# FoX/MLA hybrid layer on one core: projection tiles spread among the heads, first norm and tail reordered, and half of the output projection moved among the MLA heads

## The chip, the cores and the metric

One Trainium2 chip, one of its cores. The time is device microseconds of one execution; several runs are made and their median is given. Engines: TensorE (PE, its weight loads PEld), VectorE (DVE), ScalarE (ACT), GpSimd (POOL) and SyncE (SP), whose queue issues most transfers.

## What is computed

One inference step of one layer over T = 576 columns: 512 frames of a new stream ("prompt") and 64 frames of a running one ("sample", with 1024 cached positions). Model width 1024.

```python
z = rmsnorm(x, g_attn) @ w_in      # FoX q|k|v (512 each), forget logits (8), MLA q-latent (384), kv-latent (256), rope key (32)
fox = softmax(q k^T / 8 + F[t] - F[s], causal) v          # 8 heads x 64, F = cumsum(log sigmoid(f + b))
mla = softmax((q_lat c^T + q_rope k_rope^T) / sqrt(96), chunk-causal) c @ w_uv    # 8 heads
x = x + concat[fox, mla] @ w_out
u = causal_conv3(rmsnorm(x, g_ffn) @ w_up)
x = x + (silu(u_gate) * u_val) @ w_down                   # D_FF = 2816
y = rmsnorm(x, final_norm)
```

Outputs are y and the new state: FoX k, v and log forget values, the normalised kv-latent, the rotated key, and the last convolution rows.

## The kernel before

Everything lies transposed: features on the 128 partitions, the 576 columns along the free axis, x as eight tiles. Operands of the large products are split into a high and a low part (float32r), and a product is three matmuls: low x high, high x high, high x low. Weights come by `wload` (L183): a transfer into one of two "wr" buffers, a ScalarE copy to the high part and a subtraction for the low part (`hilo`, L192) into one of two "wh" buffers. The subtraction's engine is picked by cycling through a string of `ENG` (L54): "v" VectorE, "g" POOL; the first W0 - 1 calls go to VectorE. `gemm` (L201) works in two column halves (`HA`: 288 + 288) into two PSUM banks, so a tile of 1024 input rows is 48 matmuls. `evac` (L213) takes the two banks out on VectorE.

Buffers are named by tag with a fixed number of each: "raw" 7 (L94), "mix" 8 (L97), "xs" 8 split operands (L100), "wr" and "wh" 2; PSUM has banks g 2, s 3, t 2, o 1.

Stages:
1. x is loaded, scaled and split (`split_scaled`); the rope key with the forget logits, and the first key tile, go through TensorE while ScalarE squares x (L318). Squares are added in two groups of four by the engines of "acc0", column sums over a matrix of ones give the sum of squares, and `rstd` (L260) makes R. `consts` (L176) loads a constant block and copies its parts on VectorE. The projections are scaled by R when they are evacuated.
2. Heads come in pairs p (heads 2p, 2p+1). `fox_gemm` (L447) makes key, query and value tile of a FoX pair, three "raw" buffers. `latent` (L538) makes one of five latent tiles, `latent_norm` (L544) normalises them, `gates` (L559) makes the cumulated forget values from the logits on 8 partitions, with "raw" buffers. `mla_up` (L657) makes queries, keys and values of an MLA pair.
3. Per head: stacked operands by SyncE transfers (`stack`, L470), scores, softmax, transposes, values. Per pair: scores and values of the sample stream. Results are the eight "mix" tiles, FoX 0 to 3 and MLA 4 to 7.
4. Output projection (L859): all eight mix tiles are split, then eight tiles of 48 matmuls, added to x.
5. FFN norm (L871 to L878), 44 up-projection tiles with convolution (`up_conv`, L881), products, and down-projections in four groups; the last one in column halves of 320 and 256 (L959), each with its own norm and output transfers. Its factors are multiplied by POOL in the first half and by POOL or VectorE (`TPOOL`) in the second.

The order of stages 2 and 3 is written by five generators (`s_values`, `s_scores`, `s_sample_values`, `s_sample_scores`, `s_gemm`), each of which yields either ("after", event, latency), to wait, or ("done", cost, event), after it has emitted work. A small planner (L835) always goes on with the generator that is due first on its own clock. The program order so made sets priorities; a scheduler then orders each engine's queue by them and by when operands and buffers are expected to be free. `tc.issue_after(ins)` puts what is emitted in its block behind `ins` on the same engine.

Of the kernel before, what the change touches and what calls it, by code (L numbers as in the profile page):

```python
# [55 lines left out]
    "sq0": "a", "acc0": "gggvvv", "sq": "agv", "acc": "gvvv",  # L56
# [9 lines left out]
TPOOL = (0, 1)  # L66

W0 = 6
# [3 lines left out]
def build(nc, tc, io):  # L72
# [3 lines left out]
    psp = es.enter_context(tc.tile_pool(name="ps", bufs=1, space=PSUM))  # L76

# [5 lines left out]
    def sb(shape, dt, tag, bufs, name=None):  # L83
        return pool.tile(shape, dt, tag=tag, bufs=bufs, name=name or tag)
# [91 lines left out]
    def consts():  # L176
        nc.sync.dma_start(con[:, :N_CON], io["con"])
        V.tensor_copy(ident, con[:, K_ID:K_ID + P])
        V.tensor_copy(bfc, con[:, 0:320])
        V.tensor_copy(sel, con[0:72, K_SEL:K_SEL + 8])  # L180
# [69 lines left out]
    def rstd_of(v, y, a, out):  # L250
        S.activation(y, v, AF.Ln)
        S.activation(y, y, AF.Exp, scale=-0.5)
        newton(v, y, a, out)

    def newton(v, y, a, out):
        V.tensor_tensor(a, y, y, op=ALU.mult)
        V.scalar_tensor_tensor(a, a, -0.5, v, op0=ALU.mult, op1=ALU.mult)
        V.scalar_tensor_tensor(out, a, 1.5, y, op0=ALU.add, op1=ALU.mult)

    def rstd(ps, n, out):  # L260
        v, y, a = (raw()[:, :T] for _ in range(3))
        evac(lambda d, p, c: V.tensor_scalar(d, p, 1.0 / n, EPS, op0=ALU.mult, op1=ALU.add), v, ps)
        rstd_of(v, y, a, out)
# [52 lines left out]
    with tc.issue_after(ends[0]), tc.issue_after(ends[1]):  # L316
        consts()
        rstd(col_sums([sq_sum([t[:, :T] for t in x_in[n:n + 4]], "sq0", "acc0") for n in (0, 4)]), D, R)  # L318
# [128 lines left out]
    def fox_gemm(p):  # L447
        ps = k0 if p == 0 else in_tile(p)
        k = raw()
        evac(lambda d, p, c: V.tensor_tensor(d, p, R[:, c], op=ALU.mult), k, ps)  # L450
        G.dma_start(io["o_k"][p], k[:, :T])
        ps = in_tile(4 + p)
        q = raw()
        evac(lambda d, p, c: V.scalar_tensor_tensor(d, p, FOX_SCALE, R[:, c], op0=ALU.mult, op1=ALU.mult), q, ps)
        ps = in_tile(8 + p)
# [3 lines left out]
        return q, k, v  # L459
# [96 lines left out]
    fx = {0: fox_gemm(0)}  # L556
    gate = {}

    def gates():  # L559
        S.activation(z, z, AF.Identity, bias=bf)  # L560
        mn = raw()[:8, :T]
        V.scalar_tensor_tensor(mn, z, -1.0, z, op0=ALU.mult, op1=ALU.min)
        e = raw()[:8, :T]
        S.activation(e, mn, AF.Exp)
        up = raw()[:8, :T]
# [5 lines left out]
        logf = raw()[:8, :T]  # L571
# [4 lines left out]
        fp = raw()[:8, :T]  # L576
# [162 lines left out]

    done = {("x", 0): 0.0}  # L740
    clock = [0.0]

    def s_gemm():
        for p in range(1, 4):
            if p >= 2:
                yield ("after", ("stack", 2 * (p - 2) + 1), 0)
            fx[p] = fox_gemm(p)
            if p == 1:
                gates()
            yield ("done", 23.1, ("up", p))  # L750
            if p == 1:
                for a in range(5):
                    latent(a)
                    if a == 2:
                        rope_key()
                    if a == 1:
                        acc_c = sq_sum(craw)
                    if a == 4:
                        acc_q = sq_sum(qcr)
                    yield ("done", 7.7, ("lat", a))  # L760
            if p == 2:
                latent_norm(craw, 256, C_GKV, acc_c)
                latent_norm(qcr, 384, C_GQ, acc_q)
                for a in range(2):
                    G.dma_start(io["o_lat"][a], craw[a])
        mla_keys()
        yield ("done", 0, ("keys", 0))
        for p in range(4):
            if p == 0:
                yield ("after", ("stack", 5), 0)  # L770
            else:
                yield ("after", ("stack", 6 + 2 * p - 1), 0)
            if p % 2 == 0:
                q_rope(p // 2)
                yield ("done", 2.2, ("rope", p))
            mla_up(p)
            yield ("done", 5, ("up", 4 + p))

# [99 lines left out]
    rstd(sumsq(x2), D, R2)  # L878
    cs = sb([P, 512], F32, "KR", 1)[:, :176].rearrange("p (a b) -> p a b", b=4)

    def up_conv(ch):  # L881

        hl = wload(io["w_up"][ch], 1024)
        ps = psg()
        gemm(ps, P, hl, x2hl, HB)
# [17 lines left out]
    def g_tile():  # L903
# [9 lines left out]
        return t[0][:, k * 1152:(k + 1) * 1152].rearrange("p (a b) -> p a b", a=2)  # L913

# [44 lines left out]
    for hf, (o, w) in enumerate(HC):  # L959
# [138 lines left out]
```

## Time and profile before

| | us |
|---|---|
| median of 3 runs (lowest, highest) | 809.66 (807.43, 810.17) |
| the profiled execution | 810.69 |
| its span, first to last instruction | 808.9 |
| TensorE matmuls / weight loads busy | 772.8 / 743.3 |
| VectorE / ScalarE / POOL busy | 508.5 / 340.6 / 264.0 |

Times are microseconds from the span's start; a row of a stage table gives the length of the stretch, then each engine's busy time in it with its number of instructions. A row of a timeline gives start, duration, engine, line, operation, tiles out<-in, shapes, count, and in brackets the idle time before it and what ended it. Neighbouring instructions of one kind are merged into a row, so its duration can hold short waits. Weight loads overlap matmuls. Full clock is 1.00, the lower of the two levels 0.50.

### The profile page before, as it was taken

The page shows a single profiled execution, that of the slowest core. Times are in us where ns is not written, and L with a number is a line of the kernel's source. Part 1 is how long each engine was busy: PE and PEld are TensorE (multiplying, and loading weights), DVE is VectorE, ACT ScalarE, POOL GpSimd, SP SyncE. Part 2 cuts the span into 40 slices and gives each one's busy share as a digit, 9 for nine tenths or more (in the row PEclk, how much of TensorE's full clock was granted, in tenths as well). Part 3 has the DMA queues.
Part 4 walks back from the last instruction along what each step waited for, and adds up shares of the span by engine and source line. Part 5 has one row for each costly group of instructions (what it writes and reads, how often), then busy time and mean ns, then how long its engine had stood idle before and what let it go on. Part 6 is the DMA issues. An engine that isn't in the chain of part 4 may idle for free.

```text
span 808.9 us, 14256 instructions
## 1 busy us (share of the span) xinstructions
PE 772.8 (96%) x5582; PEld 743.3 (92%) x5582; DVE 508.5 (63%) x941; ACT 340.6 (42%) x611; POOL 264.0 (33%) x390
## 2 busy tenths in 40 slices
PE   8898999999899989999999999999999999999994
PEld 8796899897789879999999999999999999999993
DVE  6838554878677763457867524676425667675356
ACT  7224652457667864124443212343113433433231
POOL 5134342336143230223333221433222343332034
PEclk9998999999999999999999999999999999999997
DMA  9373423545563741222222223222232222222313
GB/s 329 111 212 109 109 84 106 145 107 169 129 152 80 185 131 30 80 79 79 72 85 68 79 92 105 79 79 60 79 98 80 103 80 79 79 66 83 105 40 117
DMA packets 33811, 83.98 MB, mean 104 GB/s; under 512 B 6006, under 2 KB 9350, under 8 KB 33744
## 3 DMA queue, kind: packets, MB, share of 16 engines
q1 hardware_dynamic: 31520, 78.55, 32.6%
q0 software_dynamic: 1008, 3.19, 1.1%
q10 hardware_dynamic: 1216, 1.33, 0.5%
q8 instruction: 44, 0.72, 0.4%
q14 instruction: 23, 0.19, 0.1%
HBM read 64.12 MB, written 5.49 MB: 86 GB/s over the span
## 4 chain that ended last, share of the span: by engine, by line
PE 76%; DVE 10%; ACT 5%; DMA 3%; issue 3%; SPq 1%; POOL 1%; DVEq 0%; ACTq 0%; POOLq 0%
PE g L210 31%; PE s L210 19%; PE t L210 12%; PE g L438 3%; PE g L969 1%; DMA mix<-xT 1%; DVE B L382 1%; DVE xs L267 1%; PE s L720 1%; PE t L375 1%; ACT p L326 1%; PE s L969 1%; DMA A<-qr 1%; PE s L522 1%; DVE raw L135 1%
## 5 line engine op out<-in xcount | busy, mean ns | idle before, releaser
L210 PE MATMUL g<-xs,wh 128*128 128x288 f32 (+2 forms) x2028 | 281.1, 295 | 0.3 <-ACT spt L128 0.2
L210 PEld LDWEIGHTS g<-xs,wh 128*128 128x128 f32 x2028 | 271.1, 189 | 1.7 <-ACT spt L128 0.4
L194 ACT ACTIVATE wh<-wr 128x1024 fp32r<-128x1024 f32 (+4 forms) x106 | 99.8, 942 | 204.3 <-PE g L210 88.4
L135 POOL TENSOR_TENSOR wh<-wr,wh 128x1024 fp32r<-128x1024 f32 (+3 forms) x51 | 111.8, 2192 | 216.5 <-ACT wh L194 173.7
L210 PE MATMUL s<-xs,wh 128*128 128x320 f32 (+3 forms) x840 | 121.1, 300 | 2.3 <-DVE xs L267 2.3
L210 PEld LDWEIGHTS s<-xs,wh 128*128 128x128 f32 (+1 forms) x840 | 116.3, 188 | 2.7 <-ACT wh L194 1.8
L210 PE MATMUL t<-xs,wh 128*128 128x256 f32 (+3 forms) x576 | 83.9, 296 | 1.2 <-DVE xs L267 1.2
L210 PEld LDWEIGHTS t<-xs,wh 128*128 128x128 f32 (+1 forms) x576 | 79.1, 188 | 1.6 <-DVE xs L267 1.4
L135 DVE TENSOR_TENSOR wh<-wr,wh 128x1024 fp32r<-128x1024 f32 (+5 forms) x55 | 59.0, 1077 | 13.7 <-ACT wh L194 13.4
L892 POOL COPY KR<-raw 128x2 f32<-128x2 f32 x33 | 14.6, 443 | 94.1 <-DVE raw L890 94.1
L332 POOL TENSOR_SCALAR p<-p,small 128x128 f32<-128x128 f32 (+2 forms) x48 | 27.5, 575 | 50.9 <-DVE small L327 40.8
L896 DVE SCALAR_TENSOR_TENSOR raw<-raw,par 128x578 f32<-128x578 f32 x22 | 33.6, 1526 | 14.0 <-ACT raw L895 14.0
L326 ACT ACTIVATE p<-s,small 128x128 f32<-128x128 f32 (+1 forms) x64 | 33.6, 527 | 12.5 <-DVE small L361 9.2
L920 ACT ACTIVATE raw<-raw 128x578 f32<-128x578 f32 x22 | 15.1, 688 | 54.5 <-DVE raw L897 54.5
L382 DVE TENSOR_TENSOR B<-t,B 128x512 fp32r<-128x512 f32 (+1 forms) x64 | 29.9, 482 | 9.3 <-ACT B L128 9.2
L128 ACT ACTIVATE B<-t 128x512 fp32r<-128x512 f32 (+1 forms) x64 | 26.2, 435 | 17.1 <-PE t L375 16.4
L361 DVE TENSOR_REDUCE small<-s 128x1 f32<-128x128 f32 (+1 forms) x64 | 30.5, 480 | 4.3 <-PE s L359 2.9
L896 DVE SCALAR_TENSOR_TENSOR raw<-pq,par,raw 128x578 f32<-128x578 f32 x11 | 22.7, 2059 | 12.4 <-ACT raw L895 12.4
L375 PE MATMUL t<-ident,p 128*128 128x128 f32 x160 | 29.1, 277 | 1.0 <-DVE B L382 0.5
L890 DVE TENSOR_TENSOR raw<-s,R 128x256 f32<-128x256 f32 x22 | 9.3, 424 | 31.8 <-PE s L210 31.8
L438 PE MATMUL g<-spt,sv 128*128 128x128 f32 x216 | 26.7, 276 | 0.3 <-ACT spt L128 0.2
L438 PEld LDWEIGHTS g<-spt,sv 128*128 128x128 f32 x216 | 25.2, 192 | 1.1 <-ACT spt L128 0.6
(337 smaller groups left out, 1344.1 us busy)
## 6 DMA issues: line engine op xcount, KB each, us to landing
wr<-w_up SPq DMA_DIRECT2D x44, 512.0 KB
wr<-w_dn SPq DMA_DIRECT2D x24, 384.0 KB
wr<-w_in SPq DMA_DIRECT2D x16, 512.0 KB
A<-pq SPq DMA_DIRECT2D x32, 256.0 KB
mix<-xT SPq DMA_DIRECT2D x16, 288.0 KB
wr<-w_out SPq DMA_DIRECT2D x8, 512.0 KB
A<-pq SPq DMA_DIRECT2D x24, 128.0 KB
sk<-k_c SPq DMA_DIRECT2D x4, 512.0 KB
```

What stands on the lines that cost most here:

```text
L128: S.activation(dst, src, AF.Copy)
L135: (V if pick(kind) == "v" else G).tensor_tensor(dst, a, b, op=op)
L194: S.activation(hl[:, 0, a:b], r[:, a:b], AF.Copy)
L210: PE.matmul(ps[hf][:M, :w], lhsT=hl[:, wi, kc * M:(kc + 1) * M], rhs=acts[kc][:, xi, o:o + w], start=(kc == 0 and pi == 0), stop=(kc == n ...
L326: S.activation(p, src, AF.Exp, bias=nm, accum_out=sm[:, 0:1])
L332: (G if e == "g" else V).tensor_scalar(p, p, sm[:, 1:2], 1.0, op0=ALU.mult, op1=ALU.mult)
L361: V.reduce_max(nm[:, 0:1], s[:, :W], axis=AX.X, negate=True)
L375: PE.transpose(t[:, P * (i - j):P * (i - j + 1)], st["p"][i][:, P * j:P * (j + 1)], ident)
L382: V.tensor_tensor(ptj[:, 1, off:], t[:, :w], f(ptj[:, 0, off:]), op=ALU.subtract)
L438: PE.matmul(out, lhsT=v[:, j, :], rhs=spt[:, j, :], start=(j == 0), stop=(j == 8))
L896: V.scalar_tensor_tensor(t, u[:, 1:579], par[:, C_CW + 44 + ch:C_CW + 44 + ch + 1], t, op0=ALU.mult, op1=ALU.add)
L969: PE.matmul(ps[:, :w], lhsT=whl[m][:, wi, kc * P:(kc + 1) * P], rhs=g2[kc][:, xi, c], start=(kc == 0 and pi == 0), stop=(kc == n - 1 and p ...
```

## The change

- `s_gemm` emits projection tiles one at a time, each a step of 6.4 on the planner's clock (before: a pair's three tiles at once for 23.1, a latent tile 7.7), in the order F1, two latent tiles, F2, three latent tiles, F3 (F1 is the second FoX pair). The gates come after pair 1's key tile. Both latent norms come after F3.
- The gates' small tiles are "mix" buffers instead of "raw".
- First norm: all six additions of squares on VectorE, the three constant copies behind the norm, W0 5 instead of 6.
- Output projection: after the last MLA up-projection, FoX head 7 and the fourth sample pair, `s_gemm` splits mix tiles 0 to 3 and emits eight half tiles (24 matmuls each) that add x and store the partial sum in device memory; behind the heads, eight half tiles with mix 4 to 7 load the partial sums and add them.
- FFN: the first gate tile and the first value tile run through their eight input blocks together, with the sum of squares placed after four of them.
- Tail: POOL takes four tiles of the first column half and three of the second; in the second half the factor stays in PSUM for VectorE and ScalarE copies it for POOL.

```diff
-    "sq0": "a", "acc0": "gggvvv", "sq": "agv", "acc": "gvvv",
+    "sq0": "a", "acc0": "v", "sq": "agv", "acc": "gvvv",
...
-TPOOL = (0, 1)
-W0 = 6
+TPOOL = ((0, 1, 2, 3), (0, 1, 2))
+W0 = 5
...
     def consts():
         nc.sync.dma_start(con[:, :N_CON], io["con"])
-        V.tensor_copy(ident, con[:, K_ID:K_ID + P])
-        V.tensor_copy(bfc, con[:, 0:320])
-        V.tensor_copy(sel, con[0:72, K_SEL:K_SEL + 8])
...
-        rstd(col_sums([sq_sum([t[:, :T] for t in x_in[n:n + 4]], "sq0", "acc0") for n in (0, 4)]), D, R)
+        normed = rstd(col_sums([sq_sum([t[:, :T] for t in x_in[n:n + 4]], "sq0", "acc0") for n in (0, 4)]), D, R)
+    with tc.issue_after(normed):
+        V.tensor_copy(ident, con[:, K_ID:K_ID + P])
+        V.tensor_copy(bfc, con[:, 0:320])
+        V.tensor_copy(sel, con[0:72, K_SEL:K_SEL + 8])
...
     def gates():
         S.activation(z, z, AF.Identity, bias=bf)
-        mn = raw()[:8, :T]
+        mn = mixt()[:8]
...
+    def out_half(m):
+        hl = wload(io["w_out"][m][:, :512], 512)
+        xm = mixt()
+        nc.sync.dma_start(xm, io["xT"][:, m, :])
+        ps = psg()
+        gemm(ps, P, hl, mhl[:4], HA)
+        evac(lambda d, p, c: V.tensor_tensor(d, p, d, op=ALU.add), xm, ps)
+        nc.sync.dma_start(parts[m], xm)
...
     def s_gemm():
...
+        acc = {}
+        for what in ("F1", "l0", "l1", "F2", "l2", "l3", "l4", "F3"):
+            n = int(what[1])
+            if what[0] == "F":
+                if n >= 2:
+                    yield ("after", ("stack", 2 * (n - 2) + 1), 0)
+                for j, _ in enumerate(fox_gemm(n)):
+                    if n == 1 and j == 0:
+                        gates()
+                    yield ("done", 6.4, ("part", n))
+                yield ("done", 0, ("up", n))
+            else:
+                latent(n)
...
+                yield ("done", 6.4, ("lat", n))
+        latent_norm(craw, 256, C_GKV, acc["c"])
+        latent_norm(qcr, 384, C_GQ, acc["q"])
...
             mla_up(p)
             yield ("done", 5, ("up", 4 + p))
+        yield ("after", ("o", 7), 0)
+        yield ("after", ("so", 3), 0)
+        mhl.extend(split(t) for t in mixes[:4])
+        for m in range(8):
+            out_half(m)
+            yield ("done", 3.2, ("out", m))
...
-    mhl = [split(t) for t in mixes]
+    mhl.extend(split(t) for t in mixes[4:])
     x2 = []
     for m in range(8):
-        hl = wload(io["w_out"][m], 1024)
+        hl = wload(io["w_out"][m][:, 512:], 512)
         xm = mixt()
-        nc.sync.dma_start(xm, io["xT"][:, m, :])
+        nc.sync.dma_start(xm, parts[m])
         ps = psg()
-        gemm(ps, P, hl, mhl, HA)
+        gemm(ps, P, hl, mhl[4:], HA)
...
-    rstd(sumsq(x2), D, R2)
+    def up_gemm(chs):
+        hls = [wload(io["w_up"][ch], 1024) for ch in chs]
+        pss = [psg() for _ in chs]
+        for kc in range(8):
+            if kc == 4:
+                rstd(sumsq(x2), D, R2)
+            for hl, ps in zip(hls, pss):
+                for hf, (o, w) in enumerate(HB):
+                    for pi, (wi, xi) in enumerate(((0, 1), (0, 0), (1, 0))):
+                        PE.matmul(ps[hf][:, :w], lhsT=hl[:, wi, kc * P:(kc + 1) * P], rhs=x2hl[kc][:, xi, o:o + w],
+                                  start=(kc == 0 and pi == 0), stop=(kc == 7 and pi == 2))
+        return dict(zip(chs, pss))
...
+    early.update(up_gemm((0, NCH)))
...
-        newton(v, y, a, r3)
+        if hf:
+            newton(v, y, a, pn[:, :w])
+            S.activation(r3, pn[:, :w], AF.Copy)
+            r3, r3g = pn[:, :w], r3
+        else:
+            newton(v, y, a, r3)
+            r3g = r3
...
-                if hf == 0 or m in TPOOL:
+                if m in TPOOL[hf]:
                     G.tensor_scalar(x2[m][:, c], x2[m][:, c], gl, 1.0, op0=ALU.mult, op1=ALU.mult)
-                    G.tensor_tensor(yt[:, j], x2[m][:, c], r3, op=ALU.mult)
+                    G.tensor_tensor(yt[:, j], x2[m][:, c], r3g, op=ALU.mult)
```

## Rows read from the trace of the kernel before

**Rows 1.** The page, busy time of each engine over the span.
```profile
PE 772.8 (96%) x5582; PEld 743.3 (92%) x5582; DVE 508.5 (63%) x941; ACT 340.6 (42%) x611; POOL 264.0 (33%) x390
```

**Rows 2.** Stage table: length; busy PE, PEld, DVE, ACT, POOL; PE clock, DMA share, GB/s.
```profile
20.00:41.00 21.00, 18.07 (x109) 16.01 (x109) 17.12 (x23) 6.49 (x11) 4.22 (x4) 0.92 0.37 120
...
69.00:78.00 9.00, 6.05 (x23) 4.43 (x24) 7.43 (x22) 4.68 (x11) 4.46 (x5) 0.68 0.21 66
78.00:104.00 26.00, 24.63 (x171) 21.14 (x170) 15.22 (x47) 18.29 (x49) 12.13 (x21) 0.98 0.46 111
104.00:146.00 42.00, 42.00 (x319) 41.76 (x318) 20.48 (x34) 13.01 (x24) 14.32 (x14) 1.00 0.34 101
146.00:180.00 34.00, 33.16 (x232) 30.17 (x231) 29.42 (x59) 17.82 (x38) 12.70 (x16) 1.00 0.43 121
180.00:212.00 32.00, 28.66 (x186) 23.25 (x185) 27.89 (x67) 24.50 (x66) 15.52 (x22) 1.00 0.64 170
212.00:268.00 56.00, 52.12 (x340) 46.58 (x340) 38.07 (x98) 38.16 (x95) 17.05 (x26) 1.00 0.47 121
268.00:318.00 50.00, 46.38 (x328) 41.79 (x326) 33.10 (x91) 33.02 (x84) 12.19 (x20) 1.00 0.41 114
...
369.00:381.00 12.00, 10.82 (x83) 10.62 (x83) 10.53 (x13) 5.80 (x8) 3.34 (x5) 1.00 0.19 61
```

**Rows 3.** Timelines of the first norm: DVE, ACT, POOL and PE, 13 to 31 us.
```profile
18.71 5.67 DVE L135 TENSOR_TENSOR raw<-raw 128x576 f32<-128x576 f32 x3
...
30.29 0.72 DVE L256 TENSOR_TENSOR raw<-raw 128x576 f32<-128x576 f32 x1
...
13.94 4.69 ACT L220 ACTIVATE raw<-mix 128x576 f32<-128x576 f32 x8
19.11 2.25 ACT L194 ACTIVATE wh<-wr 128x1024 fp32r<-128x1024 f32 x2 [0.48 <-PE t L210]
...
21.43 2.34 POOL L135 TENSOR_TENSOR wh<-wr,wh 128x1024 fp32r<-128x1024 f32 x1 [0.68 <-ACT wh L194]
...
24.44 3.24 PE L230 MATMUL s<-raw,ones 128*128 128x288 f32 x6 [2.89 <-DVE raw L135]
27.07 1.03 PE L210 MATMUL g<-xs,wh 128*128 128x288 f32 x2
```

**Rows 4.** Timelines of the gates: ACT, DVE, and the PE wait at their end.
```profile
35.20 0.76 ACT L560 ACTIVATE mix<-mix,bf 8x576 f32<-8x576 f32 x1
...
59.34 0.74 DVE L562 SCALAR_TENSOR_TENSOR raw<-mix 8x576 f32<-8x576 f32 x1
...
71.79 0.90 PE L523 MATMUL s<-cf,sl 72*128 72x384 f32 x3 [3.13 <-DVE cf L590]
```

**Rows 5.** Latent norms, last FoX tile and head 8's first score (PE timeline; line L548).
```profile
145.44 0.65 PE L230 MATMUL g<-raw,ones 128*128 128x288 f32 x2
...
177.98 1.85 PE L210 MATMUL g<-xs,wh 128*128 128x288 f32 x12
...
212.53 0.28 PE L701 MATMUL s<-A 128*128 128x256 f32 x1
...
L548 DVE SCALAR_TENSOR_TENSOR mix<-mix,par,raw x5: 802/805/810, 157.0 to 164.4; 128x576 f32<-128x576 f32 x5
```

**Rows 6.** Last up-projection, output projection and its evacuations; SyncE's queue.
```profile
268.17 1.64 PE L668 MATMUL g<-xs,wh 128*128 128x512 f32 x6
...
318.41 51.13 PE L210 MATMUL g<-xs,wh 128*128 128x288 f32 x384
...
L867 DVE TENSOR_TENSOR mix<-g,mix x16: 442/458/459, 323.8 to 370.2; 128x288 f32<-128x288 f32 x16
...
266.90 8.48 SPq L185 DMA_DIRECT2D wr<-w_out  x3
```

**Rows 7.** The tail: final products of VectorE (line L996), an addition of squares.
```profile
L996 DVE SCALAR_TENSOR_TENSOR pq<-mix,par,v x2: 473/706/940, 802.3 to 803.2; 128x256 f32<-128x256 f32 x2
...
796.05 1.02 DVE L978 TENSOR_TENSOR raw<-raw 128x256 f32<-128x256 f32 x1 [0.48 <-ACT raw L976]
```

More of the change, by code (lines that the diff above doesn't have):

```diff
@@ L76, in build @@
     psp = es.enter_context(tc.tile_pool(name="ps", bufs=1, space=PSUM))
+    dram = es.enter_context(tc.tile_pool(name="hbm", bufs=1, space=bass.MemoryType.DRAM))
     V, S, G, PE = nc.vector, nc.scalar, nc.gpsimd, nc.tensor
@@ L252, in rstd_of @@
         S.activation(y, y, AF.Exp, scale=-0.5)
-        newton(v, y, a, out)
+        return newton(v, y, a, out)
     def newton(v, y, a, out):
@@ L257, in newton @@
         V.scalar_tensor_tensor(a, a, -0.5, v, op0=ALU.mult, op1=ALU.mult)
-        V.scalar_tensor_tensor(out, a, 1.5, y, op0=ALU.add, op1=ALU.mult)
+        return V.scalar_tensor_tensor(out, a, 1.5, y, op0=ALU.add, op1=ALU.mult).ins
     def rstd(ps, n, out):
@@ L262, in rstd @@
         evac(lambda d, p, c: V.tensor_scalar(d, p, 1.0 / n, EPS, op0=ALU.mult, op1=ALU.add), v, ps)
-        rstd_of(v, y, a, out)
+        return rstd_of(v, y, a, out)
     def split_scaled(dst, src, g):
@@ L451, in fox_gemm @@
         G.dma_start(io["o_k"][p], k[:, :T])
+        yield
         ps = in_tile(4 + p)
@@ L454, in fox_gemm @@
         evac(lambda d, p, c: V.scalar_tensor_tensor(d, p, FOX_SCALE, R[:, c], op0=ALU.mult, op1=ALU.mult), q, ps)
+        yield
         ps = in_tile(8 + p)
@@ L458, in fox_gemm @@
         G.dma_start(io["o_v"][p], v[:, :T])
-        return q, k, v
+        fx[p] = q, k, v
+        yield
     def pair_split(q, k):
@@ L554, in split @@
         return t
-    fx = {0: fox_gemm(0)}
+    fx = {}
+    for _ in fox_gemm(0):
+        pass
     gate = {}
@@ L560, in gates @@
         S.activation(z, z, AF.Identity, bias=bf)
-        mn = raw()[:8, :T]
+        mn = mixt()[:8]
         V.scalar_tensor_tensor(mn, z, -1.0, z, op0=ALU.mult, op1=ALU.min)
-        e = raw()[:8, :T]
+        e = mixt()[:8]
         S.activation(e, mn, AF.Exp)
-        up = raw()[:8, :T]
+        up = mixt()[:8]
         V.tensor_scalar(up, e, 1.0, None, op0=ALU.add)
@@ L570, in gates @@
         V.tensor_tensor(up, up, e, op=ALU.add)
-        logf = raw()[:8, :T]
+        logf = mixt()[:8]
         V.scalar_tensor_tensor(logf, z, 0.0, up, op0=ALU.min, op1=ALU.subtract)
@@ L575, in gates @@
         G.memset(zero8, 0.0)
-        fp = raw()[:8, :T]
+        fp = mixt()[:8]
         V.tensor_tensor_scan(fp[:, :NP], logf[:, :NP], zero8[:, :NP], 0.0, op0=ALU.add, op1=ALU.add)
@@ L737, in mla_sample_values @@
         yield 0.4
+    mhl = []
+    parts = [dram.tile([P, T], F32, tag=f"part{m}", bufs=1, name=f"part{m}") for m in range(8)]
+    def out_half(m):
[6 more added lines that the diff above has]
+        nc.sync.dma_start(parts[m], xm)
     done = {("x", 0): 0.0}
@@ L743, in s_gemm @@
     def s_gemm():
[L744 to L765, printed above, removed]
+        acc = {}
[11 more added lines that the diff above has]
+                latent(n)
+                if n == 2:
+                    rope_key()
+                if n == 1:
+                    acc["c"] = sq_sum(craw)
+                if n == 4:
+                    acc["q"] = sq_sum(qcr)
+                yield ("done", 6.4, ("lat", n))
+        latent_norm(craw, 256, C_GKV, acc["c"])
+        latent_norm(qcr, 384, C_GQ, acc["q"])
+        for a in range(2):
+            G.dma_start(io["o_lat"][a], craw[a])
         mla_keys()
@@ L877, in build @@
     R2 = sb([P, T], F32, "R", 1)
-    rstd(sumsq(x2), D, R2)
     cs = sb([P, 512], F32, "KR", 1)[:, :176].rearrange("p (a b) -> p a b", b=4)
-    def up_conv(ch):
-        hl = wload(io["w_up"][ch], 1024)
-        ps = psg()
-        gemm(ps, P, hl, x2hl, HB)
+    def up_gemm(chs):
[10 more added lines that the diff above has]
+        return dict(zip(chs, pss))
+    early = {}
+    def up_conv(ch):
+        ps = early.pop(ch, None)
+        if ps is None:
+            hl = wload(io["w_up"][ch], 1024)
+            ps = psg()
+            gemm(ps, P, hl, x2hl, HB)
         u = raw()
```

## The prediction

> **What bounds the kernel now.** I read the page's busy times first: TensorE's matmuls are busy 96% of the span and its weight loads 92%, VectorE 63% [rows 1]. So TensorE is the bound, and only the time in which it does not load weights can be won. The table by stage says where that is [rows 2]. Idle weight-load time is the stretch less its PEld column: 5.0 us in 20 to 41, 4.6 in 69 to 78, 4.9 in 78 to 104, 3.8 in 146 to 180, 8.8 in 180 to 212, 9.4 in 212 to 268, 8.2 in 268 to 318, 1.4 in 369 to 381; 104 to 146 is the control, dense at 319 matmuls in 42 us (0.132 us each). The output projection is dense too, 384 matmuls in 51.13 us [rows 6]. From the stretches with idle time I went to the timelines for what is late there.
>
> [...] By the PE column the stages from 78 to 318 hold 13.1 us of idle time where PEld shows 35.1; the sum below, made from PE, would be about 15 us instead of 20.
>
> **The change, part by part.** Durations are those of the profiled execution: 810.7 us, a span of 808.9 and 1.8 around it. The median of the runs is 809.7, 1.0 lower.
>
> *First norm.* The last ScalarE square ends at 18.6 [rows 3]. Three adds on VectorE then take 5.67 us between POOL adds, though an operation of that kind and shape takes 0.72 alone [rows 3]; the column sums wait until 24.44, run at half clock (the granted clock of 20 to 41 is 0.92 [rows 2]), and the query tile of pair 0 starts only at 27.07. With all six adds on VectorE the last ends near 18.6 + 0.7 = 19.4. Next late are that tile's weights: their subtraction moves from VectorE to POOL (W0 is 5), from about 20.2, after ScalarE's copy, for 2.34 us [rows 3]; the tile starts near 22.8. **-4.3 us**; bounds 0 (POOL is held up by the norm's Newton steps) and -5. The three constant copies move behind the norm: short, and nothing before head 0 reads them. The alternation of later subtractions between POOL and VectorE shifts by one call: nothing, their number stays.
>
> *Gates and tile by tile.* ScalarE adds the forget bias at 35.20, but the next step of the chain starts at 59.34 [rows 4]. It needs a "raw" buffer, and seven are taken by q, k, v of two pairs. TensorE finally waits 3.1 us for the chain's end [rows 4]; 69 to 78 then does 23 matmuls in 9 us at a mean clock of 0.68 [rows 2], so at the lower of the two levels for most of it, after the idle stretch. With "mix" buffers (free once x is squared and split) the chain, 12.4 us from 59.34 to 71.79, starts near 31 and ends near 43, long before the next three tiles are done. The 23 matmuls cost 3.0 us at 0.132: -6.0. Heads 0 to 3 now have two tiles of pair 1 and two latent tiles beside them, where 78 to 104 had 4.9 us idle; I take two thirds, -3.2. Together **-9.2 us**; bounds -11 (no idle) and -4 (the idle time only moves). The POOL queue is passed by the o_k, o_v and o_logf stores earlier; they are issues, and POOL is busy 4.46 of 9 us there [rows 2].
>
> *Third pair ahead of three latent tiles.* Heads 4 and 5, in 146 to 180 with 3.8 us idle, get tiles beside them: -2. But the latent norms now stand behind the last FoX tile. They take from 145.44 to the last scaling near 165.2 [rows 5], 20 us that lie partly beside the last FoX tiles today; head 8's scores start at 212.53, some 33 us after the last FoX tile's matmuls ended at 179.8 [rows 5]. Heads 6 and 7 and one sample pair remain as cover. Bounds 0 and +13; I take +2, near the cover, since all inputs but the last are ready three tiles earlier. **0 us** net.
>
> *FoX half of the output projection.* 25.6 us of matmuls (half of 51.13) may go between the MLA heads. They need "xs" buffers which the latents hold until the last up-projection, ended at 269.8 [rows 6], so only the 8.2 us idle in 268 to 318 are in reach: three quarters, -6. It adds 16 more evacuations at 0.458 us [rows 6], 7.3 us on a VectorE busy 33.1 of 50 there [rows 2]: covered; without cover +7. It adds eight loads of x, eight weight issues, eight stores and eight reloads of 288 KB, 4.7 MB, on SyncE's queue, with DMA at 0.41 of its capacity in that stage [rows 2]: nothing, unless the queue blocks (a rival below). In the second half a tile is 3.2 us of matmuls instead of 6.4 while VectorE's work per tile stays: +1. **-5 us**; bounds -17 (the idle time of 212 to 268 too) and +2.
>
> *FFN norm and first two channel tiles together.* TensorE lost 1.4 us at the split of x2, in 369 to 381 [rows 2]. Four splits find their buffers earlier, and two tiles give double work per split: **-1.2 us**; bounds -1.4 and +2 (the second tile's weights come late). What is late next is the fifth split.
>
> *Tail.* Four of the first half's eight products go from POOL to VectorE; in the second half one goes from VectorE (0.47 to 0.94) to POOL [rows 7]. The VectorE adds beside POOL took up to 1.02 us at 796.05 on the end's path [rows 7]; POOL's run ends earlier, but VectorE has four more products in the same stretch. **-0.5 us**; bounds -1.5 and +1.5. [...]
>
> **Sum:** -4.3 - 9.2 + 0 - 5 - 1.2 - 0.5 = -20.2; 810.7 - 20.2 = 790.5, and against the median 789.5.
>
> **Rivals.**
> (a) *Denser than I take.* The idle 35.1 us of 78 to 318 fall to a third, -23.4, with -6.0 for 69 to 78, -4.3 and -1.2: -34.9, 774.8. For it: every stage gets filler work. Against: buffers are held late.
> (b) *VectorE becomes the bound.* It is busy 27.9 of 32 us in 180 to 212 and 29.4 of 34 in 146 to 180 [rows 2]. Then only the start and the stall are won: -4.3 - 6.0 = -10.3, 799.4. Against: in 104 to 146 it is at half.
> (c) *The halves are not among the heads.* If "xs", "wh" and "g" slots come free only after the last head, that part costs +1 instead of -5: 795.5.
> (d) *Slower: the stores block SyncE's queue.* Each store of a half waits at the head of the queue for its evacuation, and loads of head operands stand behind it. The trace has such a case: SyncE sits 8.48 us on three w_out issues and the operand loads come after [rows 6]; less the issues that is some 7.5 us. If halves are pulled ahead of the last heads' loads, three holds (22.5 us) use up the gain, four give 30.0 - 20.2 = +9.8: 819.5. Against: the planner's order puts all stacks before the first half, and transfers of the last head's operands with them.
>
> **How the numbers follow.** Forecast 0.52, (a) 0.20, (b) 0.12, (c) 0.06, (d) 0.07, and 0.03 for (d) with just under three holds, which ends near zero. Faster by over 0.3% (2.4 us, about what a measurement here can tell from no change): 0.90; within: 0.03; slower: 0.07. The range reaches to (a) and past (b): 773 to 804; outside it lie (d) and the best end of (a).
>
> **What would show it.** Right: the query tile of pair 0 starts near 23; the forget chain ends near 43 and no TensorE wait for it; no stretch below full clock between 40 and 110; head 8's scores near 200; tiles of the first half before the last head's transposes; the second half near 26 us; no wait for the x2 split. Wrong: stretches without tiles still as long, with VectorE over 90% busy (b); SyncE waiting on a store with operand loads behind it (d); norms that leave TensorE idle after the last FoX tile.

## The result, and the profile after

| | before | after |
|---|---|---|
| median, us (lowest to highest, 4 runs each) | 808.54 (807.43 to 810.17) | 841.53 (837.41 to 843.85) |
| ratio, 95% interval | | 1.0401 (1.0373 to 1.043) |
| span of the profiled execution, us | 808.9 | 842.1 |
| mean granted clock | 0.988 | 0.962 |

The change makes the kernel 4.0% slower, 33 us, where 20 us less were forecast. One execution of an experiment below (*old_order_w0_6*) took 4251.82 us, unlike its nine others (805.7 to 810.8), and is left out of its median. The page's busy times after the change answer to [rows 1]:

```profile
PE 790.0 (94%) x5582; PEld 757.3 (90%) x5582; DVE 510.1 (61%) x967; ACT 344.6 (41%) x620; POOL 255.9 (30%) x385
```

The number of matmuls is the same and every engine has a smaller share of its time. So no other engine became the bound; 33 us in which TensorE waits or runs at a lower clock came in. The stage table of the changed kernel (columns as in [rows 2]) says where:

```profile
40.00:60.00 20.00, 18.56 (x121) 16.77 (x120) 15.78 (x31) 7.83 (x14) 7.08 (x8) 0.91 0.80 216
60.00:80.00 20.00, 19.77 (x117) 16.52 (x118) 8.60 (x29) 10.35 (x27) 7.30 (x12) 0.83 0.48 120
...
140.00:180.00 40.00, 38.17 (x286) 36.11 (x285) 20.24 (x47) 18.41 (x41) 12.35 (x17) 1.00 0.23 74
180.00:200.00 20.00, 16.19 (x101) 13.47 (x99) 11.63 (x29) 6.98 (x19) 3.46 (x7) 0.95 0.48 120
200.00:220.00 20.00, 12.99 (x46) 9.41 (x46) 17.23 (x36) 13.88 (x31) 11.70 (x11) 0.53 0.25 86
220.00:240.00 20.00, 17.25 (x112) 15.63 (x111) 12.15 (x21) 9.26 (x22) 7.01 (x7) 0.91 0.41 91
240.00:260.00 20.00, 13.79 (x66) 12.46 (x64) 11.53 (x23) 9.07 (x21) 3.44 (x5) 0.83 0.55 148
```

From 180 to 260 us there are 51.0 us of weight loads in 80; 200 to 220 holds 46 matmuls at a clock of 0.53 (0.50 from 200.4 to 218.5; every clock record of the two profiled executions is 1.00 or 0.50), where the dense control of [rows 2] would hold 152. The first two rows show a loss ahead of that: 60 to 80 us is granted 0.83. The timelines name what stands in the later rows. TensorE, 186 to 251 us, columns as in [rows 3] (rows of heads 6 and 7, their sample pair and the first MLA products left out):

```profile
186.35 0.65 PE L228 MATMUL g<-raw,ones 128*128 128x288 f32 x2
...
196.38 0.81 PE L528 MATMUL s<-sk,qb 128*128 128x320 f32 x2 [3.05 <-ACT p L328]
...
205.65 0.69 PE L377 MATMUL t<-ident,p 128*128 128x128 f32 x2 [1.96 <-POOL p L334]
...
214.09 0.79 PE L392 MATMUL o<-B,v 128*128 128x256 f32 x2 [3.81 <-DVE B L384]
214.76 1.81 PE L208 MATMUL g<-xs,wh 128*128 128x288 f32 x6
216.36 0.41 PE L392 MATMUL o<-B,v 128*128 128x256 f32 x1
216.58 2.65 PE L208 MATMUL g<-xs,wh 128*128 128x288 f32 x12
...
239.32 0.28 PE L709 MATMUL s<-A 128*128 128x256 f32 x1
...
250.05 0.66 PE L729 MATMUL s<-cf,sl 96*128 96x384 f32 x1 [5.62 <-DVE cf L645]
```

and VectorE in the same time:

```profile
194.03 0.69 DVE L131 CAST sk<-wr 128x1024 fp32r<-128x1024 f32 x1 [2.74 <-DMA wr<-c_T]
194.64 0.75 DVE L254 TENSOR_TENSOR raw<-raw 128x576 f32<-128x576 f32 x1
...
208.50 4.55 DVE L554 SCALAR_TENSOR_TENSOR mix<-mix,par,raw 128x576 f32<-128x576 f32 x3
```

The latent norms' column sums start at 186.35, right behind the last FoX tile (145.44 before [rows 5]). Their first Newton step comes at 194.64, behind a cast that has waited 2.74 us for its transfer, and the last scaling ends at 213.05; the first MLA query product, 6 and 12 matmuls, starts at 214.76, head 8's first score at 239.32 (212.53 before [rows 5]). Until the query product TensorE has only heads 6 and 7 and their sample pair, which wait for their own softmax (3.05 us at 196.38, 1.96 at 205.65). Part of that wait is made by the norms: the two matmuls at 214.09 wait 3.81 us for a VectorE subtraction (L384) that is queued behind the three scalings of 4.55 us.

So most of the loss is made before head 8. The last FoX tile ends at 186.3 instead of 176.3 us, and from there to head 8 it takes 53 us instead of 36: 27 of the 33 us. Another 5 are lost between head 8's first score and the end of the output projection (162 us instead of 157); the longest wait there is the 5.62 us at 250.05.

### The profile page after: what moved, and what is told of

Its sections match the earlier page's. It is cut to its first block, busy times and chain, and to the rows that moved or that the text cites. A ratio compares the mean times of both kernels' runs of the same rounds, so it can differ in the third digit from the quotient of the medians.

```text
span 842.1 us, 14319 instructions
## 1 busy us (share of the span) xinstructions
PE 790.0 (94%) x5582; PEld 757.3 (90%) x5582; DVE 510.1 (61%) x967; ACT 344.6 (41%) x620; POOL 255.9 (30%) x385
## 4 chain that ended last, share of the span: by engine, by line
PE 77%; DVE 8%; DMA 4%; ACT 3%; issue 3%; SPq 3%; POOL 1%; POOLq 0%; ACTq 0%; DVEq 0%
PE g L208 32%; PE s L208 18%; PE t L208 12%; PE g L440 3%; PE t L377 1%; PE s L728 1%; PE g L1018 1%; PE s L528 1%; ACT wh L192 1%; DVE xs L265 1%; PE o L392 1%; PE s L1018 1%; PE g L392 1%; DVE mix L554 1%; PE g L676 1%
## 5 line engine op out<-in xcount | busy, mean ns | idle before, releaser
L192 ACT ACTIVATE wh<-wr 128x1024 fp32r<-128x1024 f32 (+4 forms) x114 | 101.4, 890 | 210.9 <-PE g L208 97.1
L208 PE MATMUL s<-xs,wh 128*128 128x320 f32 (+3 forms) x816 | 118.1, 301 | 1.1 <-DVE xs L265 1.0
L208 PEld LDWEIGHTS s<-xs,wh 128*128 128x128 f32 (+1 forms) x816 | 113.0, 188 | 1.8 <-ACT wh L192 1.2
L208 PE MATMUL t<-xs,wh 128*128 128x320 f32 (+3 forms) x552 | 80.3, 298 | 0.0
L208 PEld LDWEIGHTS t<-xs,wh 128*128 128x128 f32 (+1 forms) x552 | 76.0, 189 | 0.1
L136 DVE TENSOR_TENSOR wh<-wr,wh 128x1024 fp32r<-128x1024 f32 (+5 forms) x59 | 62.6, 1065 | 16.7 <-ACT wh L192 16.3
L384 DVE TENSOR_TENSOR B<-t,B 128x512 fp32r<-128x512 f32 (+1 forms) x64 | 30.2, 483 | 17.9 <-ACT B L129 17.3
L377 PE MATMUL t<-ident,p 128*128 128x128 f32 x160 | 32.2, 296 | 7.0 <-POOL p L334 4.0
L377 PEld LDWEIGHTS t<-ident,p 128*128 128x128 f32 x160 | 20.8, 151 | 11.2 <-POOL p L334 5.3
L392 PE MATMUL o<-B,v 128*128 128x256 f32 (+2 forms) x80 | 24.7, 380 | 4.0 <-DVE B L384 3.8
```

Of the source, the lines that this page charges most:

```text
L136: (V if pick(kind) == "v" else G).tensor_tensor(dst, a, b, op=op)
L192: S.activation(hl[:, 0, a:b], r[:, a:b], AF.Copy)
L208: PE.matmul(ps[hf][:M, :w], lhsT=hl[:, wi, kc * M:(kc + 1) * M], rhs=acts[kc][:, xi, o:o + w], start=(kc == 0 and pi == 0), stop=(kc == n ...
L377: PE.transpose(t[:, P * (i - j):P * (i - j + 1)], st["p"][i][:, P * j:P * (j + 1)], ident)
L384: V.tensor_tensor(ptj[:, 1, off:], t[:, :w], f(ptj[:, 0, off:]), op=ALU.subtract)
L392: PE.matmul(o[:, q0:], lhsT=vt[:, 2 * j + hh].rearrange("p a d -> p (a d)"), rhs=pts[j][:, a, :], start=(j == 0 and a == 0), stop=(j == 3 ...
```

## The experiments

Medians of the unchanged kernel were between 808.4 and 810.2 us in the several sets of runs, so differences between sets are uncertain by about 1 us. Theory 1 was that the norms' new place makes the loss, theory 2 that the heads of the last pair make it wherever the norms stand, theory 3 that other parts cost, too.

**Two parts of the change undone, one at a time.** *norms_before_f3* is the changed kernel with this:

```diff
-        for what in ("F1", "l0", "l1", "F2", "l2", "l3", "l4", "F3"):
+        for what in ("F1", "l0", "l1", "F2", "l2", "l3", "l4", "N", "F3"):
+            if what == "N":
+                latent_norm(craw, 256, C_GKV, acc["c"])
...
-        latent_norm(craw, 256, C_GKV, acc["c"])
```

> The changed kernel with both latent norms put between the fifth latent tile and the last FoX pair F3, as before the change they stood ahead of F3's tiles; all else as changed. Theory 1 (the norms behind F3 open a hole: from the last FoX tile to head 8's first score it is 53 us now and was 33): their 15 to 20 us lie under F3's matmuls again, head 8 starts 15 to 20 us earlier, the time is 822 to 828 us. Theory 2 (the hole comes from the heads of the last pair, which wait for VectorE and for their transfers whatever the norms do): within 5 us of the changed kernel, 837 to 845.

Measured 827.32 us, ratio 1.0229 (1.0186 to 1.0271): 14.2 us less than the change, head 8's first score at 227.7 instead of 239.3. That is theory 1 for 14.2 of the 33 us, and not for the rest. *old_order* takes the whole `s_gemm` back up to the MLA pairs (F1, five latents, F2, norms, F3) and keeps the rest of the change:

```diff
-        for what in ("F1", "l0", "l1", "F2", "l2", "l3", "l4", "F3"):
...
+        for p in range(1, 4):
...
+            for _ in fox_gemm(p):
+                pass
...
+            yield ("done", 23.1, ("up", p))
```

> The changed kernel with the old order of projections (F1 as one block, five latent tiles, F2, norms, F3, old planner costs), all else as changed, the halves of the output projection among the MLA heads too. Theory 1 (the whole loss lies in the new order of the projections): 797 to 806 us, faster than the kernel before, for the first norm and the halves then show their gain. Theory 3 (the halves, the shared buffers or the tail cost as well): 812 us or more.

815.71 us, 1.0077 (1.005 to 1.0105). The order is worth 26 us of loss, but without it the other parts, which were to give 17 us (20.2 less the 3.2 of the tiles one by one), still cost 7. Theory 3 holds beside theory 1.

**Two parts alone, on the kernel before.** *halves_only* adds `out_half` among the MLA heads and the shorter second half:

```diff
+        mhl.extend(split(t) for t in mixes[:4])
+        for m in range(8):
+            out_half(m)
+            yield ("done", 3.2, ("out", m))
...
-        gemm(ps, P, hl, mhl, HA)
+        gemm(ps, P, hl, mhl[4:], HA)
```

> The kernel before with nothing but the FoX half of the output projection moved among the MLA heads. By the prediction's term: 5 us faster, 802 to 806. By the trace of the changed kernel, where the stage from the first MLA score to the FFN lost some 5 us against the kernel before although halves lay among the heads: 808 to 815.

810.81 us, 1.0025 (1.0008 to 1.0042): nothing gained. The last sample value ends at 330.9 us instead of 318.6. TensorE's half tiles in its timeline:

```profile
287.53 1.74 PE L212 MATMUL g<-xs,wh 128*128 128x288 f32 x12
290.38 1.76 PE L212 MATMUL g<-xs,wh 128*128 128x288 f32 x12
312.94 1.82 PE L212 MATMUL g<-xs,wh 128*128 128x288 f32 x12
315.04 8.23 PE L212 MATMUL g<-xs,wh 128*128 128x288 f32 x60 [0.17 <-DVE mix L396]
327.05 3.42 PE L212 MATMUL g<-xs,wh 128*128 128x288 f32 x24
331.11 22.77 PE L212 MATMUL g<-xs,wh 128*128 128x288 f32 x168 [0.20 <-DVE mix L752]
```

120 of their matmuls run before the heads end, 16.0 us at 51.13 / 384 each [rows 6], and lengthen that stage by 12.3; half of them (60 in 8.23 us) run in one piece, not in gaps. The other 264 take until 368.4, 37.3 us, 2.1 over their rate. *first_norm_only* takes from the change the additions, the copies behind the norm and W0:

```diff
-    "sq0": "a", "acc0": "gggvvv", "sq": "agv", "acc": "gvvv",
+    "sq0": "a", "acc0": "v", "sq": "agv", "acc": "gvvv",
-W0 = 6
+W0 = 5
...
+    with tc.issue_after(normed):
+        V.tensor_copy(ident, con[:, K_ID:K_ID + P])
```

> The kernel before with nothing but the first norm's edits (all six additions on VectorE, constant copies behind the norm, W0 of 5). By the prediction's term: 4.3 us faster, 803 to 806. Rival (heads 0 and 1 wait for the forget gates at 72 us as before, so an earlier start only lengthens that wait): 808 to 811.

820.5 us, 1.014 (1.011 to 1.017): the tiles start 4 us earlier and the kernel is 12 us slower. Head 8's first score comes at 212.1, as before; the loss is behind it, in the MLA pairs, which the edits don't touch. W0 was left as a cause: it shifts by one which of the following weight subtractions POOL makes and which VectorE.

**Taking that apart, and the gates alone.** *w0_only* is one character on the kernel before:

```diff
-W0 = 6
+W0 = 5
```

> The kernel before, with W0 at 5 instead of 6 and nothing else. Theory A (the shift of the alternation costs: from here on each subtraction of a weight tile that VectorE made goes to POOL and the other way round, and the MLA pairs lose by it, as the last run lost 9 us behind head 8's first score): 815 to 821 us, head 8's first score within 2 us of 212 and the last sample value 6 to 10 us later than 318.6. Theory B (the norm's edits, an earlier start or the copies of constants, cost it): 806 to 811 us, with the last sample value near 319.

820.37 us, 1.0125 (1.0096 to 1.0154): all of the loss. Waits in TensorE's timeline that the kernel before does not have, and pieces of VectorE's and ScalarE's:

```profile
222.16 2.93 PE L668 MATMUL g<-xs,wh 128*128 128x512 f32 x6 [3.55 <-ACT raw L645]
238.22 0.47 PE L390 MATMUL o<-B,v 128*128 128x512 f32 x1 [2.13 <-DVE mix L394]
...
235.46 1.90 DVE L135 TENSOR_TENSOR wh<-wr,wh 128x512 fp32r<-128x512 f32 x1
237.39 0.69 DVE L394 TENSOR_TENSOR mix<-o,mix 64x512 f32<-64x512 f32 x1
...
219.43 1.11 ACT L636 ACTIVATE cf<-spt 32x1088 fp32r<-32x1088 f32 x1 [3.33 <-DMA spt<-kr_T]
...
221.69 0.41 ACT L645 ACTIVATE raw<-g 128x288 f32<-128x288 f32 x1
```

The second wait can be read off the shift: the subtraction of the 512-wide weights, POOL's before (1.31 us at 229.32), is now VectorE's at 235.46, beside a POOL multiplication (235.00 to 236.81). It takes 1.90 us where VectorE took 0.69 for the same shape at 207.10 in the kernel before, with POOL idle, and the addition that TensorE waits for (L394) stands behind it. The first and longer wait comes another way: the evacuation it waits for (L645, at 221.69) stands on ScalarE behind two copies, the first of which waited 3.33 us for a transfer; before, one such evacuation had gone ahead of those copies (215.18). From 205 to 320 us 665 matmuls are done instead of 731. That W0 costs the 10.2 us is shown; how they divide among such waits is not.

*norm_without_w0* is *first_norm_only* without the W0 lines of its diff:

> The kernel before with all six additions of squares on VectorE and the constant copies behind the norm, W0 left at 6. Theory A (the alternation alone costs): 803 to 808 us, the value tile of pair 0 some 3 us earlier and part of it kept to the end. Theory B (the norm's own edits cost): 816 to 822 us, as with all three edits of the first norm (820.5).

806.12 us, 0.9951 (0.9935 to 0.9967): -4.1, which with W0 at 5 is not seen. *gates_mix_only* is the kernel before with five buffers changed:

```diff
-        mn = raw()[:8, :T]
+        mn = mixt()[:8]
```

(and so for `e`, `up`, `logf`, `fp`)

> The kernel before with the gates' small tiles in the other buffers, nothing else. The prediction's step: the chain of the gates starts near 36 instead of 59 us, no wait of TensorE for it and 69 to 78 us at full clock, -3 to -6: 803 to 807 us. Rival (the gates were covered: heads wait for their stacks and for the planner's order instead, or the chain's POOL and DMA steps come later than the tiles): 808 to 811 us, with the first use of the forget values still near 68 to 72 us.

799.39 us, 0.9875 (0.9845 to 0.9905), the largest gain of the study: -10.8. Of this run, an earlier piece of VectorE's timeline, the chain's first and last steps in it, and the stage table's row of the 20 us that held the stall, first of the kernel before, then of this one:

```profile
18.73 3.52 DVE L135 TENSOR_TENSOR raw<-raw 128x576 f32<-128x576 f32 x3
...
34.45 0.74 DVE L562 SCALAR_TENSOR_TENSOR mix<-mix 8x576 f32<-8x576 f32 x1
...
47.70 1.28 DVE L590 TENSOR_TENSOR cf<-spt,cf 8x1088 fp32r<-8x1088 f32 x1
```

```profile
60.00:80.00 20.00, 16.55 (x100) 14.10 (x98) 16.79 (x39) 9.54 (x19) 7.62 (x9) 0.83 0.38 113
...
60.00:80.00 20.00, 20.00 (x152) 18.33 (x151) 13.28 (x39) 14.22 (x39) 9.91 (x17) 1.00 0.66 174
```

The chain starts 25 us earlier than in [rows 4]; no wait is left at its end, and 60 to 80 us holds 152 matmuls at full clock (before: 100, at 0.83). Not all of the gain is made there. The three additions of the first norm take 3.52 us instead of 5.67 [rows 3]; in the kernel before POOL's weight subtraction runs beside them, for 2.34 us from 21.43. Pair 1's tiles start at 37.9 us instead of 41.7, so up to 3.8 of the gain is of the kind that the prediction expected from the first norm. *after_w0_6* is the changed kernel with that line the other way round (`W0 = 6` for `W0 = 5`):

> The changed kernel with W0 at 6 instead of 5. In its other order of tiles the alternation meets other tiles, so Theory A gives a change of either sign of up to 9 us (832 to 850 us; which tiles of the MLA pairs then fall to POOL decides: better if the 384-wide query weights go to VectorE and the 512-wide to POOL as before, worse else). Theory B (alternation does not matter): 840 to 845 us, less or more by under 2.

841.57 us, 1.0386 (1.0361 to 1.041), as with 5: in the new order the shift costs nothing. Its 10 us belong to the order of before.

**Building up from the gains.** *gates_and_norm* joins the diffs of *gates_mix_only* and *norm_without_w0*; *no_order_no_halves* adds FFN start and tail (it is the changed kernel with W0 6, the diff of *old_order*, and `out_half` and its calls taken out again):

> The kernel before with the gates' small tiles in the other buffers and the first norm's edits, W0 left at 6. If the two gains (-10.8 and -4.1 us, each alone) add up: 794 to 796 us. If they are partly the same time (with the gates alone pair 0's value tile already starts at 30.0 instead of 33.8 us): 797 to 800 us.

> The changed kernel without three of its parts: planner steps and order of tiles as before, output projection whole as before, W0 at 6. What is left is gates, first norm, FFN start and tail. Prediction's terms for the last two (-1.2 and -0.5): 1 to 3 us under the run with gates and norm alone. Rival (these two cost, since the run with the old order came out some 3 us over the sum of its other parts): 1 to 4 us over it.

803.9 us, 0.9942 (0.992 to 0.9964), and 803.99, 0.9942 (0.9919 to 0.9964). The gains don't add up: with the norm's edits the time is 4.5 us over that of the gates alone. FFN start and tail are worth nothing here. *old_order_w0_6* has the halves as well (it is *old_order* with W0 6). *tiles_old_sequence* has no halves, but the tiles one at a time, steps of 6.4, in the sequence of before:

```diff
+        for what in ("F1", "l0", "l1", "l2", "l3", "l4", "F2", "N", "F3"):
...
+                for j, _ in enumerate(fox_gemm(n)):
...
+                    yield ("done", 6.4, ("part", n))
```

> The changed kernel with the order of tiles of before and W0 at 6. Theory A (with the order of before the alternation costs 10 us, in the order of the change nothing): 804 to 808 us against 815.7 with W0 at 5. Rival (the alternation costs only where the output projection is whole): 813 to 818 us. Less the run without halves it gives the price of the halves: by the run of the halves alone, 0 to +3 us.

> As the run without order and halves, but the tiles of the second and third pair and the latents emitted one at a time, in the sequence of before, each a step of 6.4, with the norms between pair 2 and pair 3. It tells the steps' size from the sequence. If the small steps gain as predicted (tiles of pair 1 beside heads 0 and 1): 3 to 8 us under the run without order and halves. If they cost (heads 0 and 1 and their stacks go ahead of pair 1's value tile, TensorE idles at half clock near 60 to 70 us as in the changed kernel, and pair 2 comes late): 3 to 12 us over it.

808.13 us, 0.9997 (0.9979 to 1.0015): the halves cost 4.1 here, and W0 7.6. And 816.98, 1.0098 (1.0073 to 1.0123): tile by tile costs 13.0, where the prediction had a gain. Its stage table from 50 to 70 us, where heads 0 and 1 now stand ahead of pair 1's value tile (67.0 instead of 49.8):

```profile
50.00:60.00 10.00, 7.80 (x41) 5.94 (x40) 9.21 (x24) 4.60 (x14) 3.96 (x5) 0.82 0.41 118
60.00:70.00 10.00, 9.96 (x57) 7.81 (x56) 5.11 (x18) 6.81 (x18) 4.14 (x7) 0.84 0.72 149
```

**What of it costs.** *f1_block* emits pair 1 in one step of 23.1 again, *latents_7_7* also has the latents' step back (7.7 for 6.4):

```diff
-                    yield ("done", 6.4, ("part", n))
+                    if n > 1:
+                        yield ("done", 6.4, ("part", n))
+                if n == 1:
+                    yield ("done", 23.1, ("part", n))
```

> As the run with tiles one at a time in the old sequence, but pair 1's three tiles in one step of 23.1, as before. If the loss arises because heads 0 and 1 go ahead of pair 1's query and value tile and run without tiles beside them: 804 to 809 us, pair 1's value tile near 57 us, the last FoX tile's end within 4 us of 168. If the steps of the later tiles cost too: 811 to 816 us.

> As the run with pair 1 in one step, with the latents' step back at 7.7; only pairs 2 and 3 are still emitted tile by tile. If the latents' smaller step shifted heads 1 to 3 against the latents: 803 to 807 us, second latent tile near 95 us. If pairs 2 and 3 cost it: 812 to 818 us.

(The tile at 57 us in the first of these texts is the first latent, pair 1's value tile starts near 50; the latent called second in the other is the third.) 816.35 us, 1.01 (1.0078 to 1.0123), and 817.59, 1.0109 (1.0076 to 1.0142): neither brings anything back. Pair 1 is back in its place (value tile at 51.4 in *f1_block*), but then the third latent tile starts at 101.4 instead of 95.3. In the timelines of *f1_block* and *no_order_no_halves* that tile starts when ScalarE has emptied a "g" bank of a sample stream's transposes (the last 0.48 and 0.19 us of idle time are put down to it). Those transposes wait for the sample stream's softmax on VectorE, whose step for the last 320 keys runs at 92.68 instead of 87.19, behind a weight subtraction, the rope key and two casts:

```profile
87.78 1.57 DVE L135 TENSOR_TENSOR wh<-wr,wh 128x1024 fp32r<-128x1024 f32 x1
89.28 0.01 DVE L304 LOAD_MASK_SELECT raw<-mix  x1
89.28 0.80 DVE L304 STREAM_SHUFFLE raw<-mix 32x576 f32<-32x576 f32 x1
89.98 0.39 DVE L383 TENSOR_TENSOR B<-t,B 128x256 fp32r<-128x256 f32 x1
90.30 1.04 DVE L306 TENSOR_TENSOR raw<-mix,raw 32x576 f32<-32x576 f32 x1
91.28 1.48 DVE L504 CAST sl<-sel 72x64 fp32r<-72x64 f32 x2
92.68 0.47 DVE L411 TENSOR_SCALAR_CACHE_REDUCE sp<-s 128x320 f32<-128x320 f32 x1
```

That is a reading of the trace of *f1_block* (VectorE's timeline above), no experiment; at head 8's first score 7.1 us of the loss are there (211.4 instead of 204.3). What the three tile-by-tile runs still share, single tiles in pairs 2 and 3 and the gates emitted ahead of pair 1's query tile, was not taken apart: which of the two costs the 13 us stays open.

*new_order_no_halves* is the changed kernel, W0 at 6, with the whole output projection; *sequence_old_steps* has of the order only the new sequence, with steps of 23.1 and 7.7 and the norms ahead of F3 (and the gates behind pair 1's key tile, as in the change); against *no_order_no_halves* its loop is

```diff
+        for what in ("F1", "l0", "l1", "F2", "l2", "l3", "l4", "N", "F3"):
...
+                yield ("done", 23.1, ("part", n))
...
+                yield ("done", 7.7, ("lat", n))
```

> The changed kernel, W0 at 6, with the output projection whole and behind the heads, as before. If the halves cost in this order as in the old one (+4.5 us): 835 to 839 us against 841.6; then the new sequence with the norms behind pair 3 has +19 to +21 of the remaining 25. If the halves fill idle time left by the new order: 842 to 850 us.

> The changed kernel without halves, W0 at 6, all steps as before (a pair 23.1, a latent tile 7.7) and the norms ahead of pair 3: only the new sequence is left, pair 2 ahead of three latent tiles. By the prediction's -2 for that: 801 to 804 us. If the latent norms, now 23 us later, delay the MLA heads: 808 to 818 us, with head 8's first score behind 210 us.

839.81 us, 1.0388 (1.0365 to 1.0411): the halves cost 1.8 here, little more than the uncertainty between sets. And 824.37, 1.0176 (1.0145 to 1.0207): pair 2 ahead of three latent tiles costs 20.4 by itself against *no_order_no_halves*. TensorE's timeline of that run, and the stage table from 140 us to the end of the last FoX tile, first of *no_order_no_halves*, then of this run:

```profile
159.42 1.46 PE L227 MATMUL g<-raw,ones 128*128 128x288 f32 x4
161.60 1.24 PE L227 MATMUL g<-raw,ones 128*128 128x288 f32 x4 [0.72 <-DVE raw L259]
166.14 22.04 PE L207 MATMUL g<-xs,wh 128*128 128x288 f32 x144 [3.31 <-DVE raw L259]
188.02 0.38 PE L342 MATMUL t<-ident,raw 128*128 128x128 f32 x2
```

```profile
140.00:167.90 27.90, 27.17 (x194) 25.14 (x194) 23.71 (x50) 15.16 (x33) 9.57 (x11) 1.00 0.43 120
...
140.00:188.00 48.00, 41.90 (x259) 38.65 (x259) 28.24 (x52) 19.98 (x43) 13.05 (x16) 0.86 0.24 74
```

Heads 4 and 5 start at 119.3 and 139.4 us (139.5 and 145.8 without the sequence), so they have run out when the last latent tile, the norms and pair 3 come: the 144 matmuls of pair 3 run from 166 to 188 with no head beside them, and the latents and norms ahead of them leave holes that nothing fills (weight loads of 38.65 in 48 us, clock 0.86). Before that the two kernels differ little: from 100 to 140 us they do 291 and 297 matmuls, so the gates' place, which differs too, is hardly where the loss is made. The last FoX tile ends at 188.0 instead of 167.9 us; behind it the two kernels take the same time to the FFN (194.7 and 195.4).

**A version below both.** *gates_and_squares* is *gates_mix_only* with `"acc0": "v"`, *gates_ffn_tail* is *gates_mix_only* with `up_gemm` and the tail's lines of the change:

> The kernel before with the gates' small tiles in the other buffers and all six additions of squares on VectorE; the constant copies stay where they were. If it is the copies behind the norm that spoil the gates' gain: 796 to 800 us. If it is the additions: 802 to 806 us.

> The kernel before with the gates' small tiles in the other buffers, the first two channel tiles together and the tail's new division; nothing else of the change. By the runs so far FFN start and tail are worth nothing: 798 to 801 us; by the prediction's terms 797 to 798.

799.06 us, 0.9887 (0.9868 to 0.9905), and 801.27, 0.9917 (0.9897 to 0.9937). The additions add nothing to the gates and take nothing away; so it is the copies of constants behind the norm that spoil the gates' gain. FFN start and tail cost 1.9 us here. With the copies (*gates_and_norm*) TensorE waits 1.50 us for a softmax at 69.33, and the stretches 60 to 80 and 80 to 100 us, with matmuls in 18.41 and 18.38 us, are granted 0.91 each; without them (*gates_and_squares*, 20.00 and 19.91 us) 1.00.

```profile
69.33 0.50 PE L516 MATMUL s<-A 128*128 128x512 f32 x1 [1.50 <-ACT p L327]
```

How the copies' place leads to this was not followed. The gates' buffers alone are the version to keep: about 10 us under the kernel before and 42 under the change.

## Why the prediction was wrong

In a row, each against the one above it (us, medians):

| kernel | time | step |
|---|---|---|
| before | 808.9 | |
| gates' buffers, first norm, FFN start, tail (*no_order_no_halves*) | 804.0 | -4.9 |
| and the new sequence, norms ahead of F3 (*sequence_old_steps*) | 824.4 | +20.4 |
| and small steps, norms behind F3 (*new_order_no_halves*) | 839.8 | +15.4 |
| and the halves (*after_w0_6*) | 841.6 | +1.8 |
| and W0 5 (the change) | 841.5 | 0 |

- *First norm.* -4.3 forecast, -4.1 measured alone. The agreement is in part luck: the forecast counted on W0 5, which was to move the first tile's weights to POOL, and the -4.1 came with W0 at 6; pair 0's query tile started at 22.2 all the same. The sentence on its side effect, that the shifted alternation "shifts by one call: nothing, their number stays", is false: in the order of before that call costs 10.2 us, though the number of subtractions stays: their place in the queues counts. In the order of the change it costs nothing, so it is not what made the change slow.
- *Gates and tile by tile.* The gates' half is right: the chain was held for a buffer, the stall goes, 60 to 80 us is granted 1.00 instead of 0.83, and with -10.8 us it gave more than the whole step, up to 3.8 of it at the first norm, where nothing was forecast from it. The other half failed: "Heads 0 to 3 now have two tiles of pair 1 and two latent tiles beside them" counted what is emitted near to what, not what is then missing later. Emitted one at a time, the tiles cost 13.0 us in the sequence of before.
- *Third pair ahead of three latent tiles.* This step failed most: 0 forecast, bounds 0 and +13, while the two steps of the table that hold it come to +35.8 with the small steps; the new sequence alone has 20.4 and the norms' place 14.2 (*norms_before_f3*), which leaves about 1 for the small steps in the new sequence. The prediction counted heads 4 and 5 as idle places to be filled and "Heads 6 and 7 and one sample pair" as cover. Both are the same supply: heads brought forward are missing behind. And the cover does not cover: from 186.3 to 212 us TensorE has 11.3 us of weight loads in 25.7 at a clock of 0.73, while two heads in a row wait for their own softmax.
- A row was misread there, too. That "the last FoX tile's matmuls ended at 179.8" was taken from the 12 matmuls at 177.98 [rows 5]. They are the second part of the first MLA query product (6 and 12 matmuls, as at 214.76 after); the FoX tile ends at 176.3, as the rows ahead of it in TensorE's timeline of the kernel before show:

```profile
167.81 8.52 PE L210 MATMUL g<-xs,wh 128*128 128x288 f32 x63
176.43 1.47 PE L210 MATMUL g<-xs,wh 128*128 128x288 f32 x6
```

Read rightly they say that the latents were ready in time for MLA work right behind the last FoX tile, and that is what the change gave up: in the change 28 us lie between the two.
- *FoX half of output projection.* -5 forecast; +2.4 alone, +4.1 and +1.8 elsewhere. The mechanism (some of it among heads) happened, with five of eight halves; what was mis-sized is the idle time that they fill, 3.7 us (16.0 less 12.3) instead of 6, and the second half lost 2.1 where 1 was taken. That would still leave a gain of 1.6, which the profiled executions show, one of each kernel (spans of 807.3 and 808.9), and the medians don't; how the rest is lost is not settled.
- *FFN norm and first two channel tiles together* and *Tail.* -1.7 forecast, +0.1 in one comparison and +1.9 in another. The last stretch did shorten a little: from the last addition of squares to the end 11.7 us, before 11.8. The final products on VectorE now take 0.47 to 0.48 each with their factor in PSUM (0.47 to 0.94 before [rows 7]). The tail gave 0.2 where 0.5 was forecast; VectorE's first product now waits 0.45 us for ScalarE's copy of the factor.
- *Rivals.* It ended on the side of (d), by another mechanism. SyncE does wait 17.72 us, on the loads of x for the halves, but behind the last head's operands. (a) did not happen, nor (c), as five of the eight halves ran among the heads; (b) neither, as VectorE is busy 17.2 us in the fullest of the 20 us stretches above. What did happen stood under "Wrong": norms that leave TensorE idle after the last FoX tile. It was given a sign, but no chance.

## What to carry to other kernels

Work that fills gaps between latency-bound chains is a supply: moving it to an earlier gap empties a later one, so a move is costed at the gap that it leaves, and a stretch of heads without tiles counts as a hole, not as cover. Before an order is changed, find in the trace what the moved result starts (here the first MLA product, right behind the last FoX tile) and count the delay from there. Run a bundle of edits part by part: five changed buffers were worth 10.8 us, and were buried under 38 us of losses.

## What was not expected of the hardware

- One character that moves no work in total (W0) costs 10.2 us in one order and nothing in another: VectorE and POOL take different times for the same subtraction of 512-wide weights (0.69 alone and 1.90 beside POOL on VectorE, 1.31 on POOL), and what stands behind it in the queue waits, as the addition at 237.39 does.
- The granted clock was lower behind some waits of TensorE: 0.50 from 73 to 79 us in the kernel before, behind the wait that ends at 71.79 [rows 4]; 0.50 from 200.4 to 218.5 in the change, behind the 3.05 us that end at 196.38; with the copies behind the norm 0.91 over 60 to 80 us, where one of 1.50 us ends at 69.33.
- The three VectorE additions of the first norm took 5.67 us in the kernel before, where POOL's weight subtraction runs beside them from 21.43 to 23.77, and 3.52 with the gates' buffers alone; in *norm_without_w0* all six on VectorE took 4.88 us, with POOL idle from 9 to 20 us.
